# A second seven-product group of columns in a two-layer decoder trunk, with weight sums moved to accumulating DMAs and squares moved to ScalarE

## The chip, the cores and the metric

The kernel runs on one core of a Trainium2 chip. The metric is the device time of one execution in microseconds, median of a few runs; lower is better.

## The reference

Two layers of a decoder trunk for 256 tokens of width 2048, in float32. Layer 0 mixes tokens with sparse attention, layer 1 with gated linear attention; each mixer is followed by a squared-ReLU MLP, and both are residual:

```python
x = x + y                                   # y: the mixer's output
h = rms_norm(x, norm_mlp[i])
x = x + jnp.square(jax.nn.relu(h @ mlp_w_up[i])) @ mlp_w_down[i]
```

`mlp_w_up` is 2048 x 8192 and `mlp_w_down` 8192 x 2048 per layer. The change is in the two MLPs alone.

## The kernel before

**Products in three parts.** Every float32 operand is split into a rounded part hi (fp32r) and a remainder lo (hi and lo tiles: `wh`, `wl` for weights), and a product is hi·hi + hi·lo + lo·hi, three matmuls. The unit in which weights are split is a half: 128 x 1024 values, a cast on ScalarE (`copy`, L194) and a subtraction on VectorE (`tt`, L198). `Weights.next` keeps the splits three halves ahead of TensorE (`AHEAD = 3`, four buffers each of `wh` and `wl`); `lows` issues the subtraction in the middle of the half before.

**The MLP (`mlp`).** The 8192 hidden columns are taken in 8 chunks of 1024. Three sorts of work, called items, are laid out in a fixed string:

- U: half of an up product for 128 hidden columns, 8 matmuls of 512 columns and 8 of 256 into a PSUM tile `psx` (`mode_b`). After the second half of each, `Up.hidden` makes the hidden values: copy out of PSUM, add the other half (`zz`), square of the positive part and the combinations (`pz`), then the split into `ht` (or, in some chunks, an `op` tile).
- C: a plain part of a down product, 12 matmuls of 512 columns (`Plain.half`, `a_half`); four of them make a block of 512 output columns for both token tiles, added to the residual `xt` by VectorE (`add`, L202).
- S: one of the seven products of Strassen's method (in Winograd's form) for two blocks of columns and two token tiles, 12 matmuls of 512 columns (`Seven.product`). Seven S take the place of eight C. Each S ends with one `add` out of its accumulator `psa`; products are chained in two accumulators: b11, t2, d2 and t4 in one, d1 and b22 in another, b21 in a third.

Chunk c of the down product and chunk c + 1 of the up product run together, in chunks 0 to 6 in the order

```python
MIX = "UUUUCCSUUSCCUUSUUSCCUUSUUSCCUUS"     # 16 U, 8 C, 7 S
```

so that two of the four column blocks are computed by seven products and two plainly. Chunk 7 has no up product beside it and is 16 C.

**Sums of weights.** The seven products need four sums of the four weight tiles a, b, c, d (1 MB each, tiles `sraw`, four places): d1 = a + b, t2 = d1 + d, d2 = t2 - a, t4 = t2 + c. VectorE makes each in one instruction over 128 x 2048 (`Group.after_lows`), in the place of b or a. The order of the products is `b11 d1 t2 b22 d2 b21 t4`. A place is loaded again by SP (`load_group`, L313) once its last half is split.

**The order of the engines' programs.** Everything is emitted by a planner (`Plan`) which keeps a modelled time per engine. Side work such as `hidden` is a generator; `W.tick`, called a few times in each item, emits its next step when the planner finds its input ready. Each engine then runs its program in the order of emission. The weights' loads are all on SP's queue; the GpSimd queue (POOL) is empty in the MLPs.

Of the kernel before, what the change touches and what calls it, by code (L numbers as in the profile page):

```python
# [18 lines left out]
P = 128  # L19
# [6 lines left out]
EPS = 1e-6  # L26
NEG = -1e30
SCALE = P ** -0.5
GELU_C = math.sqrt(2.0 / math.pi)


# [90 lines left out]
def trunk_kernel(ctx: ExitStack, tc: tile.TileContext, a: dict, out: bass.AP):  # L122
# [6 lines left out]
    def nm(s):  # L129
        uid[0] += 1  # L130
        return f"{s}_{uid[0]}"
# [60 lines left out]
    def copy(dst, src):  # L192
        W.run("act", free(src) * 0.833 + (60 if in_psum(src) else 100), [dst], [src])
        nc.scalar.copy(dst, src)  # L194

    def tt(dst, x, y, op):
        W.run("dve", free(dst) * 1.042 + 75, [dst], [x, y])
        nc.vector.tensor_tensor(dst, x, y, op=op)  # L198
# [102 lines left out]
    class Group:  # L301


        ORDER = ("b11", "d1", "t2", "b22", "d2", "b21", "t4")
        HOME = {"b11": "a", "d1": "b", "t2": "b", "b22": "d", "d2": "a", "b21": "c", "t4": "b"}

        def __init__(self, aps):
            self.aps = dict(zip("abcd", aps))
            self.raw = {}

        def load(self, slot, pool):
            raw = pool.tile([P, 2048], F32, tag="sraw", name=nm("sraw"), bufs=4)
            nc.sync.dma_start(raw, self.aps[slot])  # L313
            self.raw[slot] = raw

        def src(self, piece, half):
            return self.raw[self.HOME[piece]][:, 1024 * half:1024 * half + 1024]

        def after_lows(self, piece, half):

            a, b, c, d = (self.raw[k] for k in "abcd")
            at = (piece, half)
            if at == ("b11", 0):
                tt(b, a, b, ALU.add)
            elif at == ("d1", 1):
                tt(b, b, d, ALU.add)
            elif at == ("t2", 0):
                tt(a, b, a, ALU.subtract)
            elif at == ("b22", 1):
                tt(b, b, c, ALU.add)  # L330
                return "d"
            elif at == ("d2", 1):
                return "a"
            elif at == ("b21", 1):
                return "c"
            elif at == ("t4", 1):
                return "b"

    class Weights:
        AHEAD = 3  # L340
# [30 lines left out]
            self.half(u, 1)  # L371

        def group(self, aps):
            g = Group(aps)
            self.groups.append(g)
            self.sloads[-1] += [(g, slot) for slot in "dacb"]
            return g

        def piece(self, g, name):
# [70 lines left out]
        def lows(self):  # L450
            if self.low is None:
                return
            self.low()
            self.low = None
            h = self.halves[self.splitting]
            if len(h) == 3:
                if h[0].after_lows(h[1], h[2]):
                    self.load_group()
                return
            self.left[h[0]] -= 1  # L460
            while self.first < self.loaded and self.left[self.first] == 0:
                del self.raws[self.first]
                self.first += 1
                self.load()
# [30 lines left out]

    MIX = "UUUUCCSUUSCCUUSUUSCCUUSUUSCCUUS"

    def mlp_items(c):  # L500
        return MIX if c < 7 else "C" * 16

    def mlp_units(layer):
        weights.sloads.append([])
        us = [weights.unit(a["mlp_up"][layer, f]) for f in range(2)]
        for h in range(2):
            for f in range(2):
                weights.half(us[f], h)
        for f in range(2, 8):
            weights.both(a["mlp_up"][layer, f])  # L510
        for c in range(8):
            down = a["mlp_down"][layer, c]
            n = {"U": 0, "S": 0, "C": 0}
            g = weights.group([down[0, u] for u in range(4)]) if c < 7 else None
            u = None
            for it in mlp_items(c):
                i = n[it]
                n[it] += 1
                if it == "S":
                    weights.piece(g, Group.ORDER[i])  # L520
                elif it == "U":
                    if i % 2 == 0:
                        uu = weights.unit(a["mlp_up"][layer, 8 * (c + 1) + i // 2])
                    weights.half(uu, i % 2)
                else:
                    if i % 2 == 0:
                        first = 1 if c < 7 else 0
                        uc = weights.unit(down[first + i // 8, i // 2 % 4])
                    weights.half(uc, i % 2)
    mlp_units(0)  # L530
    for b in range(12):
# [221 lines left out]
    def mlp(prep, after, last):  # L753
        op = prep.op
        with tc.tile_pool(name="mlpz", bufs=1) as zp:
            zp.tile([P, 64], F32, tag="pad", name=nm("pad"))
            fac = {}

            def factors():
# [8 lines left out]
            def pair_tile(c, p):  # L768

                if c % 2 and p:  # L770
                    o = operand()
                    return o.rearrange("p a b t -> p (a b t)").rearrange("p (h s k) -> p h s k", h=2, k=P), o
                t = zp.tile([P, 2, 8, P], F32R, tag="ht", name=nm("ht"), bufs=5)
                return t, None

            class Up:
# [21 lines left out]
                    last_z[:] = [W.spawn(self.hidden(ps, f))]  # L798

                def hidden(self, ps, f):  # L800
                    zt = zp.tile([P, T], F32, tag="zt", name=nm("zt"), bufs=2)
                    copy(zt, ps[:, 0:T])
                    yield W.ready(zt)
                    if f % 2 == 0:
                        self.zz = zp.tile([P, 2 * T], F32, tag="zz", name=nm("zz"))
                    zz = self.zz
                    tt(zz[:, f % 2 * T:(f % 2 + 1) * T], ps[:, T:2 * T], zt, ALU.add)
                    W.give(ps, W.t["dve"])
                    if f % 2 == 0:
                        return  # L810

                    pz = zp.tile([P, 8, P], F32, tag="pz", name=nm("pz"))
                    n = 8 if "S" in mlp_items(self.c) else 4
                    stt(pz[:, 0:4, :].rearrange("p s k -> p (s k)"), zz, 0.0, zz, ALU.max, ALU.mult)
                    if n == 8:
                        both = pz[:, 0, :]
                        both = bass.AP(tensor=both.tensor, offset=both.offset,
                                       ap=[list(both.ap[0]), [3 * P, 2], [1, P]])
                        tt(pz[:, 4:6, :], both, pz[:, 1:2, :].to_broadcast([P, 2, P]), ALU.subtract)
                        stt(pz[:, 6, :], pz[:, 0, :], -1.0, pz[:, 5, :], ALU.mult, ALU.subtract)  # L820
                        stt(pz[:, 7, :], pz[:, 2, :], -1.0, pz[:, 6, :], ALU.mult, ALU.subtract)
                    ht = self.pairs[f // 2][0]
                    yield W.ready(pz)
                    copy(ht[:, 0, 0:n, :], pz[:, 0:n, :])
                    yield W.ready(ht)
                    tt(ht[:, 1, 0:n, :], pz[:, 0:n, :], ht[:, 0, 0:n, :].bitcast(F32), ALU.subtract)
# [14 lines left out]
            class Seven:  # L841


                A = {"b11": 0, "d1": 5, "t2": 6, "b22": 7, "d2": 4, "b21": 2, "t4": 3}

                def __init__(self, pairs, b):
                    self.pairs = pairs
                    self.b = b
                    self.x = self.z = None

                def product(self, i):
                    name = Group.ORDER[i]
                    if name in ("b11", "d1", "b21"):
                        W.wait({"acc": 1})
                        ps = acc1()
# [57 lines left out]

            last_z = []
            weights.pool = zp
            weights.load_group(4)
            W.spawn(factors())
            cur = Up(0)
            for f, half in [(0, 0), (1, 0), (0, 1), (1, 1)] + [(f, half) for f in range(2, 8) for half in range(2)]:
# [1 line left out]
            for c in range(8):  # L921
                items = mlp_items(c)
                nxt = Up(c + 1) if c < 7 else None
                seven = Seven(cur.pairs, 0)
                plain = Plain(c, cur.pairs, 2 if "S" in items else 0)
                n = {"U": 0, "S": 0, "C": 0}
                for it in items:
                    i = n[it]
                    n[it] += 1
                    if it == "U":  # L930
                        nxt.half(i // 2, i % 2)
                        if c == 6 and i == 15:
                            prep.free()
                    elif it == "S":
                        if i == 0:
                            hidden_done()
                        seven.product(i)
                    else:
                        plain.half(i)
                cur.free()  # L940
                cur = nxt
# [860 lines left out]
def _units_down(w):  # L1802

    v = w.reshape(2, 8, 8, P, 4, 512)
    seven = v.reshape(2, 8, 4, 2, P, 2, 2, 512).transpose(0, 1, 5, 3, 6, 4, 2, 7).reshape(2, 8, 2, 4, P, 2048)
    plain = v.reshape(2, 8, 2, 4, P, 4, 512).transpose(0, 1, 5, 2, 4, 3, 6).reshape(2, 8, 2, 4, P, 2048)
    u = plain.copy()
    u[:, :7, 0] = seven[:, :7, 0]  # L1810
    return u


# [123 lines left out]
```

## Time and profile before

| | |
|---|---|
| median of 3 runs | 2207.99 us (2207.72 to 2208.26) |
| profiled execution | 2207.57 us, span 2205.8 us |
| TensorE busy | 2193.9 us, 99% |
| VectorE busy | 1703.8 us, 77% |
| ScalarE busy | 1218.9 us, 55% |
| granted TensorE clock | 1.0 of full speed (2.4 GHz) in every slice |
| first MLP / second MLP | from about 411 us to 1112 us / from about 1513 us to the end |

A busy share is a mean over the whole span, so an engine at 77% can be near its limit in one stage; the rows below take one chunk of the second MLP by itself. Matmuls are pipelined: a row's duration is 0.39 us where the next one starts 0.23 us later, and times of items are therefore taken from start to start.

### The profile page before, as it was taken

What the parts mean: (1) busy time and instruction counts of PE and PEld (TensorE: products, weight loads), DVE (VectorE), ACT (ScalarE), POOL (GpSimd) and SP (SyncE); (2) the same over time, 40 slices, a digit from 0 to 9 for tenths busy, and PEclk for the clock granted to TensorE, in tenths of its full rate; (3) what the DMA queues carried; (4) which work ended last, traced back from release to release, by engine and by line L of the source; (5) the groups of instructions that cost most, each with busy time, mean ns of one, the idle gap of its engine ahead of it and who ended that gap; (6) DMA issues with size and microseconds to landing.
All of it is one profiled execution on the core that took longest, in us unless ns stands there. A gap on an engine that the chain in (4) does not pass through costs nothing.

```text
span 2205.8 us, 29076 instructions
## 1 busy us (share of the span) xinstructions
PE 2193.9 (99%) x11299; PEld 1851.6 (84%) x11299; DVE 1703.8 (77%) x2279; ACT 1218.9 (55%) x1906; POOL 31.2 (1%) x49
## 2 busy tenths in 40 slices
PE   8999999999999999999999999999999999999999
PEld 7888888888888888888888888888888888888887
DVE  6687676788888988988666656657888889889885
ACT  6567776555555555555566555445555555555553
POOL 0010100000000000000000000000000000000000
PEclk9999999999999999999999999999999999999999
DMA  7653442646456456464555354456464564564643
GB/s 259 219 189 134 148 178 96 251 170 224 176 197 214 170 203 218 164 218 148 196 194 176 131 183 151 156 182 255 161 230 173 205 213 171 194 227 155 226 147 142
DMA packets 62922, 410.37 MB, mean 186 GB/s; under 512 B 8256, under 2 KB 10960, under 8 KB 14912
## 3 DMA queue, kind: packets, MB, share of 16 engines
q1 hardware_dynamic: 61264, 403.78, 52.2%
q0 software_dynamic: 1520, 4.74, 0.8%
q8 instruction: 88, 1.44, 0.3%
q14 instruction: 50, 0.41, 0.1%
HBM read 405.35 MB, written 2.10 MB: 185 GB/s over the span
## 4 chain that ended last, share of the span: by engine, by line
PE 98%; DMA 1%; DVE 1%; ACT 0%; SPq 0%; issue 0%; ACTq 0%
PE psa L163 59%; PE psx L163 37%; PE psx L167 2%; DMA raw<-in_nsa_in_dram 0%; DMA xs<-in_x_dram 0%; DVE att L1665 0%; DVE wl L198 0%; SPq L1779 0%; DVE pT L198 0%; ACT wh L194 0%; ACT p L190 0%; SPq L392 0%; ACT pT L194 0%; DVE xt L202 0%; DVE g L202 0%
## 5 line engine op out<-in xcount | busy, mean ns | idle before, releaser
L198 DVE TENSOR_TENSOR wl<-raw,wh 128x1024 fp32r<-128x1024 f32 (+1 forms) x641 | 780.3, 1221 | 363.9 <-ACT wh L194 251.1
L163 PE MATMUL psa<-wh,op 128*128 128x512 f32 x2652 | 865.8, 393 | 2.5 <-ACT wh L194 2.5
L194 ACT CAST wh<-raw 128x1024 fp32r<-128x1024 f32 (+2 forms) x645 | 675.4, 1048 | 333.7 <-PE psa L163 245.3
L163 PEld LDWEIGHTS psa<-wh,op 128*128 128x128 f32 x2652 | 498.0, 188 | 107.6 <-ACT wh L194 3.4
L163 PE MATMUL psa<-wl,op 128*128 128x512 f32 x1326 | 518.0, 391 | 1.8 <-DVE wl L198 1.8
L163 PE MATMUL psx<-op,wh 128*128 128x512 f32 (+1 forms) x2080 | 517.9, 391 | 0.0
L163 PEld LDWEIGHTS psx<-op,wh 128*128 128x128 f32 (+1 forms) x2080 | 379.7, 188 | 73.3
L163 PE MATMUL psa<-wh,ht 128*128 128x512 f32 x1204 | 391.6, 390 | 0.0
L194 ACT CAST wh<-sraw 128x1024 fp32r<-128x1024 f32 x196 | 206.8, 1055 | 166.7 <-PE psa L163 154.4
L163 PEld LDWEIGHTS psx<-op,wl 128*128 128x128 f32 x2048 | 279.5, 190 | 19.9
L163 PEld LDWEIGHTS psa<-wl,op 128*128 128x128 f32 x1326 | 249.3, 188 | 49.5 <-DVE wl L198 3.7
L163 PE MATMUL psx<-op,wl 128*128 128x256 f32 x2048 | 286.0, 282 | 0.0
L163 PEld LDWEIGHTS psa<-wh,ht 128*128 128x128 f32 x1204 | 226.5, 188 | 44.2
L198 DVE TENSOR_TENSOR wl<-sraw,wh 128x1024 fp32r<-128x1024 f32 x196 | 239.4, 1221 | 25.7 <-ACT wh L194 23.6
L163 PE MATMUL psa<-wl,ht 128*128 128x512 f32 x602 | 236.7, 393 | 0.0
L194 ACT COPY zt<-psx 128x256 f32<-128x256 f32 x128 | 47.6, 372 | 283.0 <-PE psx L163 283.0
L163 PEld LDWEIGHTS psa<-wl,ht 128*128 128x128 f32 x602 | 113.4, 188 | 22.3 <-DVE wl L198 3.1
L202 DVE SCALAR_TENSOR_TENSOR xt<-psa,r,xt 128x512 f32<-128x512 f32 x170 | 123.8, 746 | 7.8 <-PE psa L163 7.8
L198 DVE TENSOR_TENSOR sraw<-sraw,sraw 128x2048 f32<-128x2048 f32 x56 | 128.1, 2288 | 0.5
L198 DVE TENSOR_TENSOR zz<-psx,zt 128x256 f32<-128x256 f32 x128 | 53.7, 420 | 9.2 <-ACT zt L194 9.2
L194 ACT CAST ht<-pz 128x1024 fp32r<-128x1024 f32 (+1 forms) x40 | 41.0, 1026 | 18.4 <-DVE pz L202 18.4
L198 DVE TENSOR_TENSOR ht<-pz,ht 128x1024 fp32r<-128x1024 f32 (+1 forms) x40 | 47.7, 1193 | 0.0
(193 smaller groups left out, 1129.9 us busy)
## 6 DMA issues: line engine op xcount, KB each, us to landing
raw<-in_mlp_up_dram SPq DMA_DIRECT2D x128, 1024.0 KB, 4.9
raw<-in_mlp_down_dram SPq DMA_DIRECT2D x72, 1024.0 KB, 4.8
sraw<-in_mlp_down_dram SPq DMA_DIRECT2D x56, 1024.0 KB, 4.9
raw<-in_gla_in_dram SPq DMA_DIRECT2D x48, 1024.0 KB, 4.8
raw<-in_nsa_in_dram SPq DMA_DIRECT2D x38, 1024.0 KB, 4.8
raw<-in_nsa_out_dram SPq DMA_DIRECT2D x16, 1024.0 KB, 4.8
raw<-in_gla_out_dram SPq DMA_DIRECT2D x16, 1024.0 KB, 4.8
xs<-in_x_dram SPq DMA_DIRECT2D x16, 128.0 KB, 6.1
```

Of the source, the lines that this page charges most:

```text
L163: nc.tensor.matmul(dst, lhsT, rhs, skip_group_check=True, **kw)
L167: nc.tensor.transpose(dst, src, idn)
L194: nc.scalar.copy(dst, src)
L198: nc.vector.tensor_tensor(dst, x, y, op=op)
L202: nc.vector.scalar_tensor_tensor(dst, x, s, y, op0=op0, op1=op1)
```

## The change

Chunks 0 to 6 compute all four column blocks by seven products (two groups; chunk 7 stays plain). The order of products becomes `b11 d1 b22 b21 t2 d2 t4`. The sums d1, t2 and t4 become accumulating DMAs from the GpSimd queue, each in two halves of 128 x 1024; d2 stays on VectorE, in halves. `sraw` gets five places instead of four, so that the b of the next group is loaded early and its d1 is formed before the present group ends. In `hidden`, the square of the positive part moves from one VectorE instruction to two on ScalarE (Relu, Square); the tile `zt` goes, and the seventh combination overwrites another, so that 7 x 128 columns are split instead of 8 x 128.

```diff
-        ORDER = ("b11", "d1", "t2", "b22", "d2", "b21", "t4")
+        ORDER = ("b11", "d1", "b22", "b21", "t2", "d2", "t4")
+        LOADS = "badc"
+        BY_DVE = ((), ())
...
+            if before is None:
+                self.places = dict(zip("abcde", range(5)))
+            else:
+                self.places = dict(zip("badce", (before.places[k] for k in "edacb")))
+                before.next = self
...
-            raw = pool.tile([P, 2048], F32, tag="sraw", name=nm("sraw"), bufs=4)
+            raw = pool.tile([P, 2048], F32, tag=f"sraw{self.places[slot]}", name=nm("sraw"), bufs=1)
...
+        def sum(self, name, half):
+            dst, src = (self.raw[k][:, 1024 * half:1024 * half + 1024]
+                        for k in {"d1": "ba", "t2": "bd", "t4": "bc", "d2": "ab"}[name])
+            if name == "d2":
+                tt(dst, src, dst, ALU.subtract)
+            elif name in self.BY_DVE[self.odd]:
+                tt(dst, dst, src, ALU.add)
+            else:
+                nc.gpsimd.dma_start(dst, src, accum_op=ALU.add)
+                W.done[W.key(dst)] = max(W.t["pe"], W.t["dve"]) + 6000.0
...
         def after_lows(self, piece, half):
-            a, b, c, d = (self.raw[k] for k in "abcd")
-            at = (piece, half)
-            if at == ("b11", 0):
-                tt(b, a, b, ALU.add)
-            elif at == ("d1", 1):
-                tt(b, b, d, ALU.add)
-            elif at == ("t2", 0):
-                tt(a, b, a, ALU.subtract)
-            elif at == ("b22", 1):
-                tt(b, b, c, ALU.add)
-                return "d"
...
+            late = "t4" in self.BY_DVE[self.odd]
+            for then in {"d1": ("t2",), "t2": ("d2",) if late else ("d2", "t4"), "d2": ("t4",) if late else ()}.get(piece, ()):
+                self.sum(then, half)
+            if half == 0:
+                return
+            if piece in ("t2", "d2"):
+                weights.load_group()
+            if piece == "d2" and self.next is not None:
+                self.next.sum("d1", 0)
+                self.next.sum("d1", 1)
+            if piece == "t4":
+                weights.load_group(2)
...
-    MIX = "UUUUCCSUUSCCUUSUUSCCUUSUUSCCUUS"
+    MIXES = {0: "C" * 16, 2: "UU" + "SUSUSUSUSUUSUS" + "SUSUSUSUSUUSUS"}
...
                 def hidden(self, ps, f):
-                    zt = zp.tile([P, T], F32, tag="zt", name=nm("zt"), bufs=2)
-                    copy(zt, ps[:, 0:T])
-                    yield W.ready(zt)
...
-                    tt(zz[:, f % 2 * T:(f % 2 + 1) * T], ps[:, T:2 * T], zt, ALU.add)
+                    z = zz[:, f % 2 * T:(f % 2 + 1) * T]
+                    copy(z, ps[:, 0:T])
+                    yield W.ready(zz)
+                    tt(z, ps[:, T:2 * T], z, ALU.add)
...
-                    stt(pz[:, 0:4, :].rearrange("p s k -> p (s k)"), zz, 0.0, zz, ALU.max, ALU.mult)
+                    act(zz, zz, AF.Relu)
+                    yield W.ready(zz)
+                    act(pz[:, 0:4, :].rearrange("p s k -> p (s k)"), zz, AF.Square)
+                    yield W.ready(pz)
...
-            weights.load_group(4)
+            first = weights.sloads[0][0][0]
+            weights.load_group(5)
+            first.sum("d1", 0)
+            first.sum("d1", 1)
```

## Rows read from the trace of the kernel before

**Rows 1.** The page's busy line, and the longest wait of TensorE.

```profile
PE 2193.9 (99%) x11299; PEld 1851.6 (84%) x11299; DVE 1703.8 (77%) x2279; ACT 1218.9 (55%) x1906; POOL 31.2 (1%) x49
...
PE psa L163 <- ACT wh L194: 2.5, 2, 1.3
```

**Rows 2.** Busy us (instructions) by engine in one chunk; clock, DMA share, GB/s.

```profile
1866.30:1952.00 85.70, 85.70 (x438) 73.11 (x438) 74.48 (x82) 46.10 (x51) 0.00 (x0) 1.00 0.57 197
```

**Rows 3.** Timeline of TensorE, first matmuls of items (start us, us).

```profile
1926.15 0.40 PE L163 MATMUL psa<-wh,ht 128*128 128x512 f32 x1
...
1934.34 1.98 PE L163 MATMUL psx<-op,wh 128*128 128x512 f32 x8
...
1939.90 0.40 PE L163 MATMUL psa<-wh,ht 128*128 128x512 f32 x1
...
1942.64 1.98 PE L163 MATMUL psx<-op,wh 128*128 128x512 f32 x8
...
1948.20 0.40 PE L163 MATMUL psa<-wh,ht 128*128 128x512 f32 x1
```

**Rows 4.** VectorE's groups in that chunk: count, busy us, mean ns, idle before.

```profile
L198 DVE TENSOR_TENSOR wl<-raw,wh 128x1024 fp32r<-128x1024 f32 x24 | 29.2, 1222 | 9.1 <-PE psa L163 7.8 <-ACT wh L194 1.3
L198 DVE TENSOR_TENSOR wl<-sraw,wh 128x1024 fp32r<-128x1024 f32 x14 | 17.1, 1222 | 1.5 <-ACT wh L194 1.4
L198 DVE TENSOR_TENSOR sraw<-sraw,sraw 128x2048 f32<-128x2048 f32 x4 | 9.1, 2287 | 0.0
L202 DVE SCALAR_TENSOR_TENSOR xt<-psa,r,xt 128x512 f32<-128x512 f32 x11 | 8.0, 746 | 0.0
L198 DVE TENSOR_TENSOR ht<-pz,ht 128x1024 fp32r<-128x1024 f32 x4 | 4.9, 1222 | 0.0
...
L202 DVE SCALAR_TENSOR_TENSOR pz<-zz 128x512 f32<-128x512 f32 x4 | 2.8, 692 | 0.1
```

**Rows 5.** VectorE's timeline around the end of a product S at 1942.64.

```profile
1941.45 1.23 DVE L198 TENSOR_TENSOR wl<-raw,wh 128x1024 fp32r<-128x1024 f32 x1 [1.54 <-PE psa L163]
1942.60 0.42 DVE L198 TENSOR_TENSOR zz<-psx,zt 128x256 f32<-128x256 f32 x1
1943.05 0.69 DVE L202 SCALAR_TENSOR_TENSOR pz<-zz 128x512 f32<-128x512 f32 x1
1943.77 0.42 DVE L198 TENSOR_TENSOR pz<-pz 128x256 f32<-128x256 f32 x1
1944.23 0.62 DVE L202 SCALAR_TENSOR_TENSOR pz<-pz 128x128 f32<-128x128 f32 x2
1944.77 1.22 DVE L198 TENSOR_TENSOR wl<-sraw,wh 128x1024 fp32r<-128x1024 f32 x1
1945.90 0.74 DVE L202 SCALAR_TENSOR_TENSOR xt<-psa,r,xt 128x512 f32<-128x512 f32 x1
```

**Rows 6.** ScalarE: casts in that chunk, and the nearest activation to Relu and Square.

```profile
L194 ACT CAST wh<-sraw 128x1024 fp32r<-128x1024 f32 x14 | 14.8, 1055 | 11.9 <-PE psa L163 11.3 <-PE psx L163 0.5
...
L190 ACT ACTIVATE junk<-xt 128x512 bf16<-128x512 f32 x24 | 15.4, 643 | 0.4
```

**Rows 7.** DMA: SBUF-to-SBUF copies from POOL (1148 to 1156 us); a saturated window.

```profile
q1 hardware_dynamic: 184, 1.25, 44.3%
q0 software_dynamic: 160, 0.52, 27.8%
...
las<-g POOLq DMA_DIRECT2D x2, 256.0 KB, 4.2
...
418.00:425.00 7.00, 7.00 (x41) 6.07 (x40) 5.17 (x12) 3.85 (x7) 0.00 (x0) 1.00 1.01 424
```

**Rows 8.** The start of the first MLP: loads, the cast that waited, its half.

```profile
411.80 2.03 SPq L313 DMA_DIRECT2D sraw<-in_mlp_down_dram  x4
...
429.87 1.05 ACT L194 CAST wh<-raw 128x1024 fp32r<-128x1024 f32 x1 [4.76 <-DMA raw<-in_mlp_up_dram]
...
434.76 2.00 PE L163 MATMUL psx<-op,wh 128*128 128x512 f32 x8
```

More of the change, by code (lines that the diff above doesn't have):

```diff
@@ L28 @@
 SCALE = P ** -0.5
+SEVENS = (2, 2, 2, 2, 2, 2, 2, 0)
 GELU_C = math.sqrt(2.0 / math.pi)
@@ L301, in trunk_kernel, with __init__ @@
     class Group:
-        ORDER = ("b11", "d1", "t2", "b22", "d2", "b21", "t4")
+        ORDER = ("b11", "d1", "b22", "b21", "t2", "d2", "t4")
         HOME = {"b11": "a", "d1": "b", "t2": "b", "b22": "d", "d2": "a", "b21": "c", "t4": "b"}
-        def __init__(self, aps):
+        LOADS = "badc"
+        BY_DVE = ((), ())
+        def __init__(self, aps, before):
+            self.odd = 0 if before is None else 1 - before.odd
             self.aps = dict(zip("abcd", aps))
+            if before is None:
[3 more added lines that the diff above has]
+                before.next = self
+            self.next = None
             self.raw = {}
         def load(self, slot, pool):
-            raw = pool.tile([P, 2048], F32, tag="sraw", name=nm("sraw"), bufs=4)
+            raw = pool.tile([P, 2048], F32, tag=f"sraw{self.places[slot]}", name=nm("sraw"), bufs=1)
             nc.sync.dma_start(raw, self.aps[slot])
             self.raw[slot] = raw
+        def sum(self, name, half):
[8 more added lines that the diff above has]
+                W.done[W.key(dst)] = max(W.t["pe"], W.t["dve"]) + 6000.0
         def src(self, piece, half):
@@ L319, in after_lows @@
         def after_lows(self, piece, half):
-            a, b, c, d = (self.raw[k] for k in "abcd")
-            at = (piece, half)
-            if at == ("b11", 0):
-                tt(b, a, b, ALU.add)
-            elif at == ("d1", 1):
-                tt(b, b, d, ALU.add)
-            elif at == ("t2", 0):
-                tt(a, b, a, ALU.subtract)
-            elif at == ("b22", 1):
-                tt(b, b, c, ALU.add)
-                return "d"
[L332 to L337, printed above, removed]
+            late = "t4" in self.BY_DVE[self.odd]
[10 more added lines that the diff above has]
+                weights.load_group(2)
     class Weights:
@@ L373, in group @@
         def group(self, aps):
-            g = Group(aps)
+            g = Group(aps, self.groups[-1] if self.groups else None)
             self.groups.append(g)
-            self.sloads[-1] += [(g, slot) for slot in "dacb"]
+            self.sloads[-1] += [(g, slot) for slot in Group.LOADS]
             return g
@@ L456, in lows @@
             if len(h) == 3:
-                if h[0].after_lows(h[1], h[2]):
-                    self.load_group()
+                h[0].after_lows(h[1], h[2])
                 return
@@ L494, in trunk_kernel @@
     out_units(a["nsa_out"])
-    MIX = "UUUUCCSUUSCCUUSUUSCCUUSUUSCCUUS"
+    MIXES = {0: "C" * 16, 2: "UU" + "SUSUSUSUSUUSUS" + "SUSUSUSUSUUSUS"}
     def mlp_items(c):
-        return MIX if c < 7 else "C" * 16
+        return MIXES[SEVENS[c]]
     def mlp_units(layer):
         weights.sloads.append([])
+        weights.groups = []
         us = [weights.unit(a["mlp_up"][layer, f]) for f in range(2)]
@@ L513, in mlp_units @@
             n = {"U": 0, "S": 0, "C": 0}
-            g = weights.group([down[0, u] for u in range(4)]) if c < 7 else None
-            u = None
             for it in mlp_items(c):
@@ L519, in mlp_units @@
                 if it == "S":
-                    weights.piece(g, Group.ORDER[i])
+                    if i % 7 == 0:
+                        g = weights.group([down[i // 7, u] for u in range(4)])
+                    weights.piece(g, Group.ORDER[i % 7])
                 elif it == "U":
@@ L526, in mlp_units @@
                     if i % 2 == 0:
-                        first = 1 if c < 7 else 0
-                        uc = weights.unit(down[first + i // 8, i // 2 % 4])
+                        uc = weights.unit(down[SEVENS[c] + i // 8, i // 2 % 4])
                     weights.half(uc, i % 2)
@@ L755, in mlp @@
         with tc.tile_pool(name="mlpz", bufs=1) as zp:
-            zp.tile([P, 64], F32, tag="pad", name=nm("pad"))
+            zp.tile([P, 32], F32, tag="pad", name=nm("pad"))
             fac = {}
@@ L772, in pair_tile @@
                     return o.rearrange("p a b t -> p (a b t)").rearrange("p (h s k) -> p h s k", h=2, k=P), o
-                t = zp.tile([P, 2, 8, P], F32R, tag="ht", name=nm("ht"), bufs=5)
+                t = zp.tile([P, 2, 7, P], F32R, tag="ht", name=nm("ht"), bufs=5)
                 return t, None
@@ L810, in hidden @@
                         return
-                    pz = zp.tile([P, 8, P], F32, tag="pz", name=nm("pz"))
-                    n = 8 if "S" in mlp_items(self.c) else 4
-                    stt(pz[:, 0:4, :].rearrange("p s k -> p (s k)"), zz, 0.0, zz, ALU.max, ALU.mult)
-                    if n == 8:
+                    yield W.ready(zz)
+                    pz = zp.tile([P, 7, P], F32, tag="pz", name=nm("pz"))
+                    act(zz, zz, AF.Relu)
+                    yield W.ready(zz)
+                    act(pz[:, 0:4, :].rearrange("p s k -> p (s k)"), zz, AF.Square)
+                    yield W.ready(pz)
+                    n = 7 if "S" in mlp_items(self.c) else 4
+                    if n == 7:
                         both = pz[:, 0, :]
@@ L820, in hidden @@
                         stt(pz[:, 6, :], pz[:, 0, :], -1.0, pz[:, 5, :], ALU.mult, ALU.subtract)
-                        stt(pz[:, 7, :], pz[:, 2, :], -1.0, pz[:, 6, :], ALU.mult, ALU.subtract)
+                        stt(pz[:, 1, :], pz[:, 2, :], -1.0, pz[:, 6, :], ALU.mult, ALU.subtract)
                     ht = self.pairs[f // 2][0]
@@ L841, in mlp @@
             class Seven:
-                A = {"b11": 0, "d1": 5, "t2": 6, "b22": 7, "d2": 4, "b21": 2, "t4": 3}
+                A = {"b11": 0, "d1": 5, "t2": 6, "b22": 1, "d2": 4, "b21": 2, "t4": 3}
                 def __init__(self, pairs, b):
@@ L849, in __init__, with product @@
                     self.x = self.z = None
-                def product(self, i):
-                    name = Group.ORDER[i]
+                def product(self, name):
                     if name in ("b11", "d1", "b21"):
@@ L923, in mlp @@
                 nxt = Up(c + 1) if c < 7 else None
-                seven = Seven(cur.pairs, 0)
-                plain = Plain(c, cur.pairs, 2 if "S" in items else 0)
+                plain = Plain(c, cur.pairs, 2 * SEVENS[c])
                 n = {"U": 0, "S": 0, "C": 0}
@@ L936, in mlp @@
                             hidden_done()
-                        seven.product(i)
+                        if i % 7 == 0:
+                            seven = Seven(cur.pairs, 2 * (i // 7))
+                        seven.product(Group.ORDER[i % 7])
                     else:
@@ L1809, in _units_down @@
     u = plain.copy()
-    u[:, :7, 0] = seven[:, :7, 0]
+    for c, n in enumerate(SEVENS):
+        u[:, c, :n] = seven[:, c, :n]
     return u
```

## The prediction

> **What bounds the kernel now.** I read the page's first part, then TensorE's waits, then one chunk by itself. TensorE is busy 99% of the span, and its longest wait comes to 2.5 us in all [rows 1]. In one chunk of 85.7 us it shows 85.7 us of work, VectorE 74.5 us (87%) and ScalarE 46.1 us (54%), at full clock [rows 2]. So the MLPs end by TensorE's instruction count, with VectorE 11 us a chunk behind it. A removed matmul is worth its full time as long as nothing new makes TensorE wait, and the question is how much of VectorE's slack the change uses up, and where.
>
> **TensorE's part.** The start-to-start times of items [rows 3]: a product S took 1942.64 - 1939.90 = 2.74 us. From 1926.15 to 1934.34 one S and two C took 8.19 us, so a C is (8.19 - 2.74)/2 = 2.725 us. Two U took 1939.90 - 1934.34 = 5.56 us, one 2.78. A chunk now has 16 U, 8 C and 7 S: 44.5 + 21.8 + 19.2 = 85.5 us. The change puts seven S in the place of eight C: 19.2 for 21.8, or 2.62 us less, leaving 82.8 us. With 7 chunks in each of 2 layers this is 14 x 2.62 = **36.7 us less**. That S takes the same time between two U is seen in the rows: this one stood between U's.
>
> **VectorE's part**, by chunk. Instructions in a row overlap by 0.09 us (the split at 1944.77 lasts 1.22, the next starts at 1945.90, 1.13 later [rows 5]), so I take each row's mean less 0.09 [rows 4]. Added: 14 S have 28 splits, 7 S and 8 C had 22, so 6 x 1.13 = 6.8 us; d2 twice in two halves, 4 x 1.13 = 4.5; residual adds, 14 for 11, 3 x 0.66 = 2.0. Removed: four sums of 2.20, 8.8; four squares of 0.72 (start to start in [rows 5]), 2.9; an eighth of four `ht` subtractions, 0.6. Sum: 74.5 + 13.3 - 12.3 = 75.5 us of 82.8, or 91% instead of 87%. The moved work pays for the added splits and no more. On the average this is hidden behind TensorE; it costs nothing as long as no single wait is tight (below).
>
> **ScalarE's part.** 6 more casts of 1.055 and eight activations which I price by the nearest row at 0.643 (512 columns out of SBUF) [rows 6]: 46.1 + 6.3 + 5.1 = 57.5 of 82.8 us, 69%. Hidden behind TensorE. Against this move speaks the Trainium skill, ScalarE: Activation LUTs, Rules for kernel authors, which sends relu and products to VectorE; the trace agrees on the price of the pair itself (0.69 us in one instruction there, 1.29 us in two here). By that rule the squares would stay and VectorE would hold 78.4 of 82.8 us; the sum for TensorE would be the same, so I follow the engines' busy times, which put the slack on ScalarE.
>
> **The sums as DMAs.** 6 DMAs of 128 x 1024 floats (0.524 MB) in a group, 12 in a chunk, 168 in all, on a POOL queue with nothing else in the MLPs. No row shows an accumulating DMA. Bounds for what one takes of the 16 engines: at least its bytes at the rate of a saturated window, 0.524 MB at 424 GB/s = 1.24 us; the nearest row, plain SBUF copies from POOL, took 27.8% of 8 us, 2.2 us, for the same bytes; twice that, since an accumulation reads two operands, is 4.4 us [rows 7]. I take 2.5 us, two passes at the saturated rate. The loads of a chunk are 197 GB/s x 85.7 us = 16.9 MB [rows 2], 39.8 us at 424 GB/s. Together 39.8 + 12 x 2.5 = 70 of 82.8 us: hidden, with 15% to spare.
>
> Who waits for a sum: ScalarE's cast of the piece that uses it, with every cast behind it, and SP's load of a place that it reads. Between the splits of d1 and t2 lie U, b22, U, b21 and U, 13.8 us of TensorE; between d2 (after which the next group's d1 is issued) and the next d1 lie U, t4, b11 and U, 11.0 us. A 256 KB copy landed in 4.2 us; twice the bytes and two reads add up to 3.3 us, 7.5 us in all, and the second half of a d1 comes up to 4.4 us later, at 12 us. This is just over the 11.0 us, and the casts run three halves (some 5 us) ahead of TensorE. Cost taken: 0. SP's own queue is not held, since each place is loaded again only after a split that already waited for the sum.
>
> **The start of each MLP.** Before, the first cast that needs a load queued behind the four `sraw` loads waited 4.76 us for it and ended at 430.92; TensorE used it at 434.76, so 3.8 us were to spare [rows 8]. A fifth load adds 1.05 MB, 2.5 us at 424 GB/s, and the two halves of d1 add 2.5 to 8.8 us if they go ahead of it. TensorE so waits 0 to 7.5 us per layer. I take 1, near the low end, since d1 needs two loads first and shares the engines with the rest: **2 us more**.
>
> **The new order of products.** d2 and t4 add into the same accumulator as t2, b22 into that of d1. With the new order only one U, 2.78 us, stands between d1 and b22 and between d2 and t4, where two U or more stood before. TensorE can't start b22 before VectorE has added d1 into `xt` out of that bank. In [rows 5] the add after the S that ended at 1942.64 ended at 1946.64, 4.0 us later. So the wait is between 0 and 1.2 us at 2 x 28 = 56 places. Ahead of that add stood the square (0.72) and the two `pz` steps (1.0 us, 1943.77 to 1944.77). The square leaves VectorE, and what follows it now comes two ScalarE steps (1.3 us) later, most likely behind the add: 4.0 - 1.7 = 2.3 us, under 2.78. I take 0.05 us per place for the times it doesn't fit: **3 us more** (0 to 67).
>
> **Sum:** 2207.57 - 36.7 + 2 + 3 = 2175.9, against the profiled execution, which is 0.4 us under the median of 2207.99; that is within the noise, and I say **2176 us**.
>
> **Rivals.**
>
> 1. *TensorE waits for the accumulator.* For it: VectorE at 91% and the 4.0 us of [rows 5]. Against it: the square leaves, and VectorE idled 1.54 us before that stretch. At 1.2 us in each of 56 places the time is 2171 + 67 = 2238, slower. It decides at 0.65 us per place: over that the 36.7 us are gone. Partly, 0.2 to 0.5 us per place, it gives 2182 to 2199.
> 2. *The DMA engines become the bound.* At 4.4 us per half sum a chunk needs 39.8 + 53 = 92.6 us of DMA, 9.8 more than TensorE's: 2171 + 137 = 2308, slower. It decides at (82.8 - 39.8)/12 = 3.6 us per half sum and is slower than before from 3.8. For it: the nearest row, doubled. Against it: the engines were busy 72% of that row's window (44.3 and 27.8, [rows 7]), so it prices a queue with gaps, not a full one. The Trainium skill, DMA: Bandwidth & Descriptors, Issuing engines are not separate DMA queues, says that DMAs of all issuers run on the same 16 engines. By that rule the sums come straight out of the loads' share, as reckoned here; no row shows the two in a saturated window.
> 3. *The sums land late or VectorE falls behind in bursts.* Half a microsecond per half sum on half of the 168 is 42 us, which would leave 2213; I find a third of that more likely, some 10 to 20 us, 2181 to 2195. It speaks against it that three halves are split ahead.
>
> That the products aren't saved can be excluded: the new string has 14 S and no C.
>
> **How the numbers follow.** A measurement of this kernel can tell 0.2% (4.4 us) from no change. Forecast (2169 to 2181): 0.56. Rival 1 in part 0.16, in full 0.06. Rival 2: 0.10. Rival 3: 0.08. A mixture which ends within 4.4 us of before: 0.04. So faster 0.56 + 0.16 + 0.08 = 0.80, same 0.04, slower 0.16. The range goes from 2169 (the bare TensorE sum, 2170.9, less noise and rounding of the items) to 2201, where the partial cases end; it leaves out the full rivals and the mixture, 0.20.
>
> **What would show it.** Right: TensorE about 82.8 us per chunk and still busy throughout; VectorE near 75.5; half sums landing within 11 us; adds after d1 and d2 ending within 2.8 us of the product. Wrong: waits `psa <- DVE xt` at b22 and t4 (rival 1); DMA share at 1.0 and casts waiting for `raw` or `sraw` (rival 2); casts of d1, t2, t4 waiting for POOL's DMAs with the DMA share below 1 (rival 3); a wait of the first U's of an MLP of more than a microsecond or two.

## The result and the profile after

The changed kernel takes 2220.33 us in the median of 9 runs (2212.44 to 2230.72) against 2207.35 us before (9 runs, 2206.91 to 2208.26): a ratio of 1.0061, 95% interval 1.0048 to 1.0074. It is slower by 0.6%, where 2176 us was forecast. The spread is new as well: 18 us between its runs, 1.4 us between those of before. The profiled execution is the fastest of them, 2212.44 us with a span of 2210.7 us; its rows show less than a run in the median lost.

The busy line of the page and TensorE's three largest groups of waits (us in total, times, longest us), which answer to [rows 1]:

```profile
PE 2173.5 (98%) x11131; PEld 1827.6 (83%) x11131; DVE 1711.9 (77%) x2341; ACT 1362.3 (62%) x2118; POOL 175.2 (8%) x217
...
PE psa L165 <- DVE xt L204: 12.9, 10, 2.0
PE psx L165 <- ACT wh L196: 7.6, 2, 3.9
PE psa L165 <- ACT zz L196: 6.0, 12, 0.5
```

The 168 matmuls are gone (11299 to 11131), and TensorE's busy time fell by 20 us, but it now waits in the MLPs, where it never did: for the residual add (`DVE xt`), for two casts, and 12 times for something that the profile puts down to `ACT zz`.

One chunk of the second MLP, and then DMA in the same stretch (queue: packets, MB, share of 16 engines; issues: count, KB, median us to landing). They answer to [rows 2] and [rows 7]:

```profile
1653.30:1737.10 83.80, 83.29 (x426) 70.88 (x425) 75.22 (x87) 55.73 (x64) 10.25 (x12) 1.00 0.92 278
...
q0 software_dynamic: 1749, 6.38, 40.2%
...
raw<-in_mlp_up_dram SPq DMA_DIRECT2D x8, 1024.0 KB, 9.4
sraw<-in_mlp_down_dram SPq DMA_DIRECT2D x8, 1024.0 KB, 11.3
sraw<-sraw POOLq DMA_DIRECT2D x12, 512.0 KB, 9.3
```

A chunk with few waits is 1.9 us shorter than the 85.7 us of before. VectorE holds 75.2 us of it and ScalarE 55.7. The DMA engines are busy 92%, and in the median the loads take about twice as long to land as on the page of before:

```profile
raw<-in_mlp_up_dram SPq DMA_DIRECT2D x128, 1024.0 KB, 4.9
```

**The start of an MLP** (timeline; SP's, POOL's, ScalarE's and TensorE's rows, in answer to [rows 8]):

```profile
412.53 2.62 SPq L326 DMA_DIRECT2D sraw<-in_mlp_down_dram  x5
415.25 28.35 SPq L419 DMA_DIRECT2D raw<-in_mlp_up_dram  x4
...
422.80 1.82 POOL L337 DMA_DIRECT2D sraw<-sraw  x2 [111.14 <-DVE zz L200]
...
438.47 1.04 ACT L196 CAST wh<-raw 128x1024 fp32r<-128x1024 f32 x1 [11.45 <-DMA raw<-in_mlp_up_dram]
...
432.69 2.00 PE L165 MATMUL psx<-op,wh 128*128 128x512 f32 x8
434.53 1.11 PE L165 MATMUL psx<-op,wl 128*128 128x256 f32 x8
439.57 2.92 PE L165 MATMUL psx<-op,wh 128*128 128x512 f32 x8 [3.93 <-ACT wh L196]
442.29 1.90 PE L165 MATMUL psx<-op,wl 128*128 128x256 f32 x8
```

The cast that had waited 4.76 us waits 11.45, and TensorE stands for 3.93 us. The 8 matmuls after it take 2.72 us to the next row (439.57 to 442.29), where the 8 at 432.69 take 1.84. The granted clock behind this wait and behind that of the second MLP (columns as in [rows 2]; the clock is the third number from the end):

```profile
439.57:445.00 5.43, 5.43 (x21) 4.68 (x22) 5.43 (x7) 4.42 (x7) 0.00 (x0) 0.69 0.59 210
1544.25:1551.00 6.75, 6.75 (x22) 5.70 (x23) 6.52 (x8) 5.70 (x9) 0.00 (x0) 0.58 0.67 242
```

A part of each stretch ran at the lower clock, 1.2 GHz: 5.43 us at 0.69 and 6.75 us at 0.58 come to some 1.7 and 2.8 us lost, an estimate. With the two waits, 3.93 and 3.71 us, the starts cost this execution some 12 us.

**A late sum** (timeline; POOL, ScalarE, VectorE, TensorE):

```profile
1769.67 1.19 POOL L337 DMA_DIRECT2D sraw<-sraw  x1
...
1786.21 1.05 ACT L196 CAST wh<-sraw 128x1024 fp32r<-128x1024 f32 x1 [2.17 <-DMA sraw<-sraw]
...
1787.29 1.23 DVE L200 TENSOR_TENSOR wl<-sraw,wh 128x1024 fp32r<-128x1024 f32 x1 [2.01 <-ACT wh L196]
...
1793.83 0.74 DVE L204 SCALAR_TENSOR_TENSOR xt<-psa,r,xt 128x512 f32<-128x512 f32 x1
...
1789.13 0.39 PE L165 MATMUL psa<-wl,ht 128*128 128x512 f32 x1
...
1790.28 1.98 PE L165 MATMUL psx<-op,wh 128*128 128x512 f32 x8
1792.10 1.11 PE L165 MATMUL psx<-op,wl 128*128 128x256 f32 x8
1794.72 0.47 PE L165 MATMUL psa<-wh,ht 128*128 128x512 f32 x1 [1.52 <-DVE xt L204]
```

Read from the top: the second half of a d1 is issued at 1769.67 and lands at 1786.2. ScalarE's cast waits 2.17 us for it, VectorE's next split 2.01 us for ScalarE. Everything after it on VectorE, which then works without a gap, is late, among it the add of the d1 product, which ended on TensorE at 1790.28: the add ends at 1794.57, 4.3 us later. One U stands between, and TensorE can't start b22 in that accumulator before 1794.72. No TensorE instruction waited for the late weights themselves, but little was left of the three halves by which they are to be ahead: the late split ended at 1788.52 and TensorE first read it at 1789.13.

**The last product of a chunk** (timeline; VectorE, ScalarE, TensorE):

```profile
1649.52 0.75 DVE L204 SCALAR_TENSOR_TENSOR xt<-psa,r,xt 128x512 f32<-128x512 f32 x1
...
1649.96 0.37 ACT L196 COPY zz<-psx 128x256 f32<-128x256 f32 x1 [1.15 <-PE psx L165]
...
1647.00 1.98 PE L165 MATMUL psx<-op,wh 128*128 128x512 f32 x8
1648.82 1.11 PE L165 MATMUL psx<-op,wl 128*128 128x256 f32 x8
1650.42 0.48 PE L165 MATMUL psa<-wh,ht 128*128 128x512 f32 x1 [0.49 <-ACT zz L196]
```

Here no sum is late: d2 ended at 1647.00, its add at 1650.27, 3.3 us later, and t4 starts at 1650.42. The copy `zz` only ended last by the records; e10 below tells that the add was the cause.

### The profile page after: what moved, and what is told of

It reads as the page before. It is cut to its first block, busy times and chain, and to the rows that moved or that the text cites. A ratio compares the mean times of both kernels' runs of the same rounds, so it can differ in the third digit from the quotient of the medians.

```text
span 2210.7 us, 29776 instructions
## 1 busy us (share of the span) xinstructions
PE 2173.5 (98%) x11131; PEld 1827.6 (83%) x11131; DVE 1711.9 (77%) x2341; ACT 1362.3 (62%) x2118; POOL 175.2 (8%) x217
## 4 chain that ended last, share of the span: by engine, by line
PE 94%; DMA 3%; DVE 1%; ACT 1%; issue 0%; SPq 0%; DVEq 0%; ACTq 0%
PE psa L165 58%; PE psx L165 35%; DMA raw<-in_mlp_up_dram 2%; PE psx L169 2%; DMA sraw<-sraw 1%; ACT wh L196 0%; DVE wl L200 0%; DMA raw<-in_nsa_in_dram 0%; DVE xt L204 0%; SPq L326 0%; ACT zz L196 0%; DVE att L1690 0%; DVE pT L200 0%; DVE zz L200 0%; SPq L1804 0%
## 5 line engine op out<-in xcount | busy, mean ns | idle before, releaser
L200 DVE TENSOR_TENSOR wl<-raw,wh 128x1024 fp32r<-128x1024 f32 (+1 forms) x529 | 642.2, 1220 | 252.1 <-ACT wh L196 248.2
L196 ACT CAST wh<-raw 128x1024 fp32r<-128x1024 f32 (+1 forms) x533 | 557.3, 1047 | 311.9 <-PE psa L165 245.3
L200 DVE TENSOR_TENSOR wl<-sraw,wh 128x1024 fp32r<-128x1024 f32 x392 | 475.4, 1222 | 123.5 <-ACT wh L196 115.5
L196 ACT CAST wh<-sraw 128x1024 fp32r<-128x1024 f32 x392 | 408.7, 1048 | 164.5 <-PE psa L165 89.8
L165 PE MATMUL psa<-wh,ht 128*128 128x512 f32 x1128 | 387.0, 396 | 19.2 <-DVE xt L204 12.9
L337 POOL DMA_DIRECT2D sraw<-sraw x168 | 144.0, 942 | 1306.9 <-DVE wl L200 560.2
L204 DVE SCALAR_TENSOR_TENSOR xt<-psa,r,xt 128x512 f32<-128x512 f32 x212 | 157.6, 746 | 7.9 <-PE psa L165 7.9
L196 ACT COPY zz<-psx 128x256 f32<-128x256 f32 x128 | 47.7, 373 | 153.6 <-PE psx L165 153.6
L200 DVE TENSOR_TENSOR sraw<-sraw,sraw 128x1024 f32<-128x1024 f32 x56 | 68.3, 1220 | 0.0
L200 DVE TENSOR_TENSOR zz<-psx,zz 128x256 f32<-128x256 f32 x128 | 53.8, 420 | 10.2 <-ACT zz L196 9.2
L196 ACT CAST ht<-pz 128x896 fp32r<-128x896 f32 (+1 forms) x40 | 37.1, 927 | 25.3 <-DVE pz L204 24.5
## 6 DMA issues: line engine op xcount, KB each, us to landing
sraw<-in_mlp_down_dram SPq DMA_DIRECT2D x112, 1024.0 KB, 11.2
```

Source lines behind the costliest of these rows:

```text
L165: nc.tensor.matmul(dst, lhsT, rhs, skip_group_check=True, **kw)
L204: nc.vector.scalar_tensor_tensor(dst, x, s, y, op0=op0, op1=op1)
L337: nc.gpsimd.dma_start(dst, src, accum_op=ALU.add)
```

## The experiments

Theory A, formed from these rows: TensorE loses its gain at two places, at the start of each MLP (loads and the first d1 ahead of the up products' weights) and at the accumulators, where b22 follows d1 and t4 follows d2 with one U between, so that any lateness of VectorE's add is TensorE's. Its rivals: B, the DMA engines are the bound by their bytes; C, VectorE's queue is.

**e1: the start's loads later.**

```diff
-            weights.load_group(5)
-            first.sum("d1", 0)
-            first.sum("d1", 1)
...
                 cur.half(f, half)
+                if f >= 1 and f <= 5 and half == 1:
+                    weights.load_group(1)
+                if f == 4 and half == 1:
+                    first.sum("d1", 0)
+                    first.sum("d1", 1)
```

> The five group loads of each MLP's start are issued one by one after up products 1 to 5, and the first d1 after product 4, instead of all ahead of the first up product; all else as in the changed kernel. Theory A (lateness: a sum or load that lands late holds ScalarE's cast, VectorE behind it, and TensorE by the accumulator): the two waits of 3.9 and 3.7 us at the start and the half-clock stretches behind them go, so 9 to 13 us less than the changed kernel's 2220, some 2208 to 2211, and the other waits stay. Theory B (the 16 DMA engines are the bound by bytes): the same bytes in the same MLP, the time is only moved, 2217 to 2222. Theory C (VectorE's queue is the bound): the start is not its place, 2215 to 2221.

Measured: 2207.02 us (12 runs, 2201.21 to 2219.35), ratio to before 1.0002 (0.9988 to 1.0016). 13.3 us less than the changed kernel, just past the end of A's range; the waits `psx <- ACT wh` of the start are gone from its profile, the other waits are not:

```profile
PE psa L165 <- DVE xt L204: 17.1, 13, 2.0
PE psa L165 <- ACT zz L196: 5.5, 11, 0.5
```

**e2: no accumulating DMAs.**

```diff
-                nc.gpsimd.dma_start(dst, src, accum_op=ALU.add)
-                W.done[W.key(dst)] = max(W.t["pe"], W.t["dve"]) + 6000.0
+                pass
```

> The sums d1, t2 and t4 are left out (no accumulating DMA at all; the split of these pieces reads the plain weights, so the output is not the reference's); every TensorE, VectorE and ScalarE instruction stays. Theory A: no sum can be late, so the accumulator waits of 1.2 to 2.1 us behind a late d1 or t4 go (some 13 us in the profiled run, more in the others), and the start is shorter; those of 0.65 us at each chunk's last product stay: 2187 to 2200. Theory B: 88 MB fewer through the DMA engines, also 2185 to 2200. Theory C: the same work for VectorE, 2214 to 2221.

Measured: 2174.52 us (2173.85 to 2174.71), ratio 0.9849 (0.9836 to 0.9862); 12.5 us below the low end of A's and 10.5 below that of B's. No wait of TensorE is left in either MLP, also none at t4, which A had put down to VectorE alone, and none at the start, though the five loads still go ahead there. C falls: with the whole of VectorE's work the kernel runs at TensorE's pace. This is also the bare worth of the removed products: 2207.57 - 2174.52 = 33.1 us.

**e3: b22 and t4 in accumulators of their own.**

```diff
-                    if name in ("b11", "d1", "b21"):
+                    if name in ("b11", "d1", "b22", "b21"):
...
-                        ps = self.x if name in ("t2", "d2", "t4") else self.z
-                    fresh = name in ("b11", "d1", "b21")
+                        ps = self.x if name in ("t2", "d2") else self.z
+                    fresh = name in ("b11", "d1", "b22", "b21", "t4")
...
-                    if name in ("b22", "b21", "t4"):
+                    if name in ("d1", "b22", "d2", "t4"):
                         W.give(ps, W.t["dve"])
```

> b22 is added up in an accumulator of its own, and t4 in that of b21, both started afresh (d1 is missing in b22's block and t2 and d2 in t4's, so the output is not the reference's); nothing else changes, the sums are still DMAs. Theory A: no product waits for VectorE's read of an accumulator one U earlier, so most of the 23 us of such waits go, except where a late cast holds TensorE by itself: 2195 to 2207. Theory B: the waits come back as waits for casts, 2214 to 2222. Theory C: likewise, 2212 to 2220, with waits for wl.

Measured: 2186.76 us (2186.55 to 2188.25), ratio 0.9906 (0.9894 to 0.9919), 33.6 us less than the changed kernel and 8 below the low end of A's range. Its sums land as late as before (second halves of d1 in the second MLP after 15.3 us in the median from the end of their issue, 15.1 in the changed kernel), and ScalarE waits for them as long:

```profile
PE psx L165 <- ACT wh L196: 6.8, 2, 3.8
PE psa L165 <- ACT wh L196: 2.3, 2, 1.5
...
ACT wh L196 <- DMA sraw<-sraw: 31.4, 17, 3.7
```

ScalarE waited 31.4 us for sums (26.9 in the changed kernel), yet of TensorE's waits the start's 6.8 us are nearly all that is left. The spread is smaller too, 1.7 us over four runs.

**e4: one U moved between the groups.**

```diff
-    MIXES = {0: "C" * 16, 2: "UU" + "SUSUSUSUSUUSUS" + "SUSUSUSUSUUSUS"}
+    MIXES = {0: "C" * 16, 2: "U" + "SUSUSUSUSUUSUS" + "U" + "SUSUSUSUSUUSUS"}
```

> One of the two U at the head of a chunk is moved between its two groups, so that every d1 has U, t4, U, b11, U (13.8 us) after the issue of its sum, where the second group's had 11.0 and the first's 16.6; same work. Theory A: the second half of d1, which landed 15.1 us after its issue and held 11 of the 14 late casts, is just in time, so 8 to 14 us less than 2220: 2206 to 2212; a new wait could come at the chunk's head, where the hidden values have one U less. Theory B: same bytes, 2217 to 2222. Theory C: same work, 2216 to 2222.

Measured: 2216.85 us (2214.98 to 2219.82), ratio 1.0042 (1.0029 to 1.0055): only 3.5 us less, a miss for A and inside C's range. No cast waits for a sum any more, but:

```profile
PE psa L165 <- ACT zz L196: 12.0, 24, 0.5
PE psx L165 <- ACT wh L196: 6.8, 2, 3.8
PE psa L165 <- DVE ht L200: 3.2, 8, 0.4
PE psa L165 <- DVE op L200: 2.4, 6, 0.4
```

The half-microsecond wait before t4 now stands in both groups (24 instead of 12), and the head of a chunk waits for its hidden values (`ht`, `op`), as the expectation had named. Time for the sums alone doesn't do it.

**e5: separate accumulators and two more adds.** On top of e1 and e3's edit the missing terms are added from the accumulators that hold them:

```diff
-                    for t, k, sign in {"b11": [(0, 0, 0)], "d1": [(1, 1, 1)], "t2": [(0, 1, 1)], "b22": [(0, 1, 1)],
-                                       "d2": [(1, 1, 1)], "b21": [(0, 0, 0)], "t4": [(1, 0, 0)]}[name]:
+                    for t, k, sign in {"b11": [(0, 0, 0)], "d1": [(1, 1, 1), (0, 1, 1)], "t2": [(0, 1, 1)], "b22": [(0, 1, 1)],
+                                       "d2": [(1, 1, 1), (1, 0, 0)], "b21": [(0, 0, 0)], "t4": [(1, 0, 0)]}[name]:
```

> With the later start of e1, b22 has an accumulator of its own and t4 starts afresh in that of b21, and the residual takes d1 and the sum b11 + t2 + d2 by one more add each (56 adds of 0.66 us on VectorE); the computation is whole again. Theory A (a late cast costs TensorE only through an accumulator that VectorE has still to read): 2174 plus what the extra 2.6 us per chunk of VectorE (94% of a chunk) cost, 2174 to 2184, with waits for wl at most. Theory C (VectorE's queue is the bound): 37 us of work more on it, 2200 to 2215.

Measured: 2176.27 us (2173.94 to 2177.28), ratio 0.9858 (0.9844 to 0.9873). This beats both kernels, by 30.9 us and by 44. VectorE does 31 us more than in the changed kernel, and TensorE's longest wait is back at the size of [rows 1]:

```profile
PE 2162.6 (99%) x11131; PEld 1821.1 (84%) x11131; DVE 1742.5 (80%) x2397; ACT 1357.3 (62%) x2118; POOL 175.2 (8%) x217
...
PE psa L165 <- DVE wl L200: 2.4, 5, 0.8
```

**e6: e1 and e3 together.** The edits are those above.

> e1 and e3 together (b22 and t4 without the terms of the other products, so the output is not the reference's; the sums land as late as before and move the same bytes). Theory A: both places where lateness reaches TensorE are gone, so it comes to the time without any sums, 2173 to 2178. Theory B (bytes and contention on the DMA engines cost something by themselves): it stays above that by 5 us or more, 2180 to 2190.

Measured: 2175.60 us (2174.62 to 2175.81), ratio 0.9855 (0.9839 to 0.9872). Against B: with all 168 accumulating DMAs it is 1.1 us over e2, which has none. ScalarE waits 37.1 us for sums here, more than anywhere above, and it costs nothing:

```profile
ACT wh L196 <- DMA sraw<-sraw: 37.1, 20, 3.0
```

**e7: the squares back on VectorE**, on top of e1.

```diff
-                    yield W.ready(zz)
...
-                    act(zz, zz, AF.Relu)
-                    yield W.ready(zz)
-                    act(pz[:, 0:4, :].rearrange("p s k -> p (s k)"), zz, AF.Square)
-                    yield W.ready(pz)
+                    stt(pz[:, 0:4, :].rearrange("p s k -> p (s k)"), zz, 0.0, zz, ALU.max, ALU.mult)
```

> e1 with the square of the positive part back on VectorE in one instruction (32 of 0.69 us per layer, 2.9 us more per chunk on VectorE, 5.1 less on ScalarE). Theory A with the squares as a help: the add of d1 and d2 stands behind 0.7 us more on VectorE, so 5 to 20 us over e1's 2207: 2212 to 2227. The other way (the hand-over VectorE to ScalarE and back holds ScalarE's casts): faster than e1, 2195 to 2204.

Measured: 2227.86 us (2222.26 to 2229.44), ratio 1.0089 (1.0074 to 1.0104), 20.8 us over e1 and 0.9 past A's range. The move to ScalarE is a gain of its own, and by the same way: with 2.9 us more per chunk in VectorE's queue the adds are later, and TensorE's waits for them are 30.3 us where e1 had 17.1, or 22.6 with the 5.5 us named `ACT zz`, which e9 and e10 show to be waits for an add too:

```profile
PE psa L165 <- DVE xt L204: 30.3, 22, 4.2
```

**e8: all sums on VectorE**, on top of e1.

```diff
-        BY_DVE = ((), ())
+        BY_DVE = (("d1", "t2", "t4"), ("d1", "t2", "t4"))
```

> e1 with the three sums d1, t2 and t4 back on VectorE in halves (12 more instructions of 1.13 us per chunk, 13.6 us), no accumulating DMA; two seven-product groups as in the change. VectorE would hold 89 us of a chunk where TensorE holds 83, and a d1 on VectorE may wait there for its load: theories A and C both say slower than before, 2250 to 2320; under 2230 would mean that the DMAs cost more than they save.

Measured: 2372.18 us (2370.94 to 2372.80), ratio 1.0747 (1.0731 to 1.0763), 52 us above the range. The DMAs pay. The mean granted clock was 0.972 in its profile, and TensorE waits for VectorE at the accumulators and at the splits:

```profile
PE psa L165 <- DVE xt L204: 97.9, 52, 4.2
PE psx L165 <- DVE wl L200: 28.8, 24, 1.8
```

How much of the 165 us is VectorE's load, the wait of a d1 for its load in VectorE's queue, or the clock, this run doesn't divide.

**e9 and e10: one accumulator each**, on top of e1: in e9 b22 alone gets its own with one more add, in e10 t4 alone (the halves of e5's edit).

> e1 with b22 alone in an accumulator of its own and one more add after d1; t4 still follows d2 in theirs. In e1's profile 11 waits before b22 (all in a chunk's second group, behind a late second half of d1) held 14.6 us, 14 before t4 8.2 us. Theory A (late d1 through b22): 15 to 22 us less than e1, 2185 to 2193. If d2 to t4 is the place instead: 2198 to 2206.

> e1 with t4 alone started afresh in b21's accumulator and one more add after d2; b22 still follows d1. Theory A: only the 8 us before t4 go, and with them a little of what follows: 8 to 14 us less than e1, 2193 to 2199. If d2 to t4 is the place instead: 2183 to 2190.

Measured: e9 2187.80 us (2185.74 to 2188.85), ratio 0.9911 (0.9898 to 0.9924); e10 2196.10 us (2191.72 to 2199.53), ratio 0.9945 (0.9933 to 0.9957). From e1 that is 19.2 and 10.9 us, 30.1 in sum, where both together (e5) give 30.8: the two places add up. In e9 the 12 waits named `ACT zz` stay; in e10 they are gone, and those named `DVE xt` stay. So the former are waits for d2's add:

```profile
PE psa L165 <- ACT zz L196: 6.0, 12, 0.5
```

(e9), and

```profile
PE psa L165 <- DVE xt L204: 17.0, 12, 2.0
```

(e10).

**e11: e5 with the early start.**

> The changed kernel with both separate accumulators and the two more adds, but with its own start (five loads and d1 ahead of the up products). Theory A: e5 and the start's 11 to 13 us, 2185 to 2190, as e3 with parts left out. If the start costs less where nothing else waits: 2177 to 2183.

Measured: 2188.43 us (2186.30 to 2190.42), ratio 0.9915 (0.9902 to 0.9928): 12.2 us over e5, so the start costs about the same with and without the other waits.

## Why the prediction was wrong

Its sum was 2207.57 - 36.7 + 2 + 3. The runs give -33.1 (e2) + 13.3 (e1 against the changed kernel) + 31.4 (e6 against e1) = 11.6, or 2219.2 of the 2220.3 measured. These runs form a chain, so the sum has to close but for the 1.1 us of e6 over e2; that each cost stands by itself is shown by other pairs. The start costs 11.2 us between e3 and e6 and 12.2 between e11 and e5, the accumulators 33.6 us between the changed kernel and e3.

- **TensorE's part**, -36.7: the mechanism was right and the size a tenth off, -33.1. In the changed kernel a product S took 2.76 us (1664.39 to 1667.15, its neighbours below), where 2.74 was taken from a single one; over 14 S in 14 chunks that would be some 4 us. More items say the same: of those without a wait beside them, 40 S between two U took 2.75 us before in the median and 146 took 2.77 after. Up to its last chunk each MLP of e2 is 17.1 us shorter than before, 2.44 a chunk where 2.62 was forecast, and the last chunk is up to 0.5 us longer. Why an S is longer is open.

```profile
1661.62 1.98 PE L165 MATMUL psx<-op,wh 128*128 128x512 f32 x8
1664.39 0.39 PE L165 MATMUL psa<-wh,ht 128*128 128x512 f32 x1
1667.15 1.07 PE L165 MATMUL psx<-op,wh 128*128 128x512 f32 x4
```

- **VectorE's and ScalarE's loads**: 75.5 and 57.5 us per chunk forecast, 75.2 and 55.7 measured. Right, and not the question.
- **What a half sum takes of the DMA engines**: 2.5 us forecast; 40.2% of 83.8 us over 12 is 2.8 us. Within the bounds, and rival 2 didn't come to pass: e6 against e2 is 1.1 us. The Trainium skill, DMA: Bandwidth & Descriptors, Issuing engines are not separate DMA queues, says that DMAs of all issuers interleave on the same 16 engines; this trace agrees (loads landed in 9.4 and 11.3 us here, in 4.9 before), but it became a matter of lateness, not of the sum of bytes.
- **The sums' lateness, cost taken 0**: this step failed in its logic. The landing of a second half of d1 was forecast at 12 us, against a stretch of 11.0 us, and measured at 15.1 (16.4 from the start of the issue, as the page counts); 11.0 us holds for a chunk's second group alone, the first has 16.6. The prediction then wrote it off against the three halves by which casts run ahead. That reserve did protect TensorE's weights, by 0.6 us in the rows above. But the cast stands in ScalarE's queue, the split behind it in VectorE's, and behind that the add which frees the accumulator. The reserve of the weights is not a reserve of the adds.
- **The new order of products, 3 us**: the step that decides. The place and the 56 sites were right; the value taken, 0.05, was not: 31.4/56 = 0.56 us in the mean. The deciding price of 0.65 us leaned on the other terms; with 33.1 and 13.3 in their place it is (33.1 - 13.3)/56 = 0.35. The add was forecast to end 2.3 us after its product, inside the U of 2.78; in the rows above it ended after 3.3 us where no sum was late, and after 4.3 where one was. In e1's profile, 31.5 us over e6's, 24 of the 56 places wait, 22.6 us by the rows; the last section says what the rest is. It was argued from a single stretch with its square taken out, and without the lateness of the step before; the two were priced apart, and they act in series (rival 3 feeds rival 1). e9 and e10 put 19.2 us at b22, where most waits stand behind a late d1, and 10.9 at t4, which e2 shows to depend on the sums as well. The full rival 1, said to be slower than before, had a chance of 0.06.
- **The start, 2 us** of 0 to 15: measured 13.3, 6.6 per MLP. The delay of the load was within the bounds (the cast ends 8.6 us later than before, though the up products start only 0.7 us later), but the value was taken near the low end on the ground that d1 shares the engines; sharing is what delays the load: e2, with the five loads but without d1's sum, doesn't wait there. The lower clock after the waits, some 4.5 us in the profiled execution, was not in the sum at all.
- **The squares on ScalarE**: said to leave TensorE's sum the same if undone, though the step on the new order counted on the square being gone; e7 shows 20.8 us. The busy times said that the engine choice didn't matter, the queue in front of the add said that it did.

## What to carry to other kernels

Work running ahead for one input doesn't cover the others: list for each instruction of the critical engine every buffer that it needs, those that it overwrites included, and ask who frees them and what stands in front of that in its queue. When products are chained in one accumulator with a read between, the distance between read and next write is a deadline for the reading engine; a fresh accumulator and one more add of 0.66 us bought, in the mean of 56 places, 0.55 us on TensorE, from an engine with time to spare. And before a saving is written off as lost to a busy DMA or engine, take the wait away and see: here the 92% busy DMA engines cost about 1 us.

## What was not expected of the hardware

- After a TensorE wait of 3.7 us came a stretch at the lower clock. The window around the one in the second MLP (columns as in [rows 2]) has a mean granted clock of 0.71, between the levels of 2.4 and 1.2 GHz; nothing like it is in the profiles of e5 and e6, which don't wait there and show a mean of 1.0.

```profile
1540.00:1547.50 7.50, 3.79 (x13) 2.92 (x12) 3.27 (x4) 4.34 (x7) 0.00 (x0) 0.71 0.92 345
```

- Shorter waits at the accumulators did the same at times. In e1's profile a wait of 1.96 us before 943.75 was followed by such a stretch, and so was one of 1.93 us before 769.46; waits of 1.91 and 1.95 us (before 857.57 and 1957.01) were not, and what tells them apart is open:

```profile
940.68 1.11 PE L165 MATMUL psx<-op,wl 128*128 128x256 f32 x8
943.75 0.47 PE L165 MATMUL psa<-wh,ht 128*128 128x512 f32 x1 [1.96 <-DVE xt L204]
944.06 0.39 PE L165 MATMUL psa<-wl,ht 128*128 128x512 f32 x1
...
943.50:949.50 6.00, 5.75 (x18) 4.63 (x19) 4.62 (x6) 2.10 (x2) 0.00 (x0) 0.72 0.77 249
```

  In each stretch 6.00 us at 0.72 are some 1.7 us lost, 3.4 in the two. The row also counts the wait too short: the 8 matmuls at 940.68 usually take 0.95 us to the next (a U of 2.77 less 1.82 for its first 8, in the rows further up), so 2.12 us were lost before 943.75, and 0.08 more until 944.06 (0.31 us where 0.23 is usual): 2.20 in all, 0.24 more than the row's 1.96. If all 24 waits are short by as much, an estimate, 22.6 + 3.4 + 5.8 = 31.8 us stand against the 31.5 between the profiles of e1 and e6.

- The accumulating DMA of 0.52 MB occupied the DMA engines for 2.8 us, against 2.2 us of the nearest row, a plain copy of as many bytes; it didn't cost double. Its bytes are counted once in the profile (12 sums in 6.38 MB).
- The runs' spread of 18 us goes with the accumulator waits: e3 and e6, which differ from the changed kernel and from e1 only there, spread over 1.7 and 1.2 us in four runs each, with the sums landing as late as ever.
